# Hymba layer on one core: every on-chip tile begins on a multiple of 64 bytes of its partition

## The chip, the cores and the metric

The kernel runs on 1 core of one Trainium2 chip. The metric is device time in microseconds (us), the median of several runs; less is better. The engines are PE (TensorE, with PEld for its weight loads), DVE (VectorE), ACT (ScalarE), POOL (GpSimd) and SP (SyncE, which issues all DMAs here).

## What is computed

One layer on 2,048 rows of 1,024 float32 values: differential attention (4 heads) beside an HGRN2 recurrence (4 heads), an output projection, then a feed-forward part with a short convolution.

```python
h = _rmsnorm(x, ln1_w[l])
proj = h @ w_in[l]
dq, dk, dv, hq, hf, hi, hg = jnp.split(proj, offs, axis=-1)
...
o_diff = _diff_attention(dq, dk, dv, lam, lam_init, diff_subln_w[l])
...
o_hgrn = _hgrn2(hq, hf, hi, hg, lb, hgrn_norm_w[l])
x = x + jnp.concatenate([o_diff, o_hgrn], axis=-1) @ w_out[l]
x = x + _conv_ffn(_rmsnorm(x, ln2_w[l]), w_up[l], conv_w[l], conv_b[l], w_down[l])
```

`_conv_ffn` multiplies by `w_up` (1,024 x 5,632), convolves one half over 3 rows, applies silu, multiplies by the other half and then by `w_down` (2,816 x 1,024).

## The kernel before, in words

Every large product is made of three matmuls: each float32 operand is split into a high part and a remainder (`split` and `halves`, an ACT cast and a subtraction on DVE or POOL; the subtraction is line 582), and high x high, high x low and low x high are summed in PSUM. In `PE.matmul(dst, lhsT, rhs)`, lhsT is the stationary operand, loaded as weights, and rhs the moving one, streamed past it. The trace names a matmul `dst<-rhs,lhsT`.

There are four stages.
- **Mixer** (lines 157 to 485): four passes `s`, one for each pair of heads, each over eight blocks of 256 rows. `proj_a` multiplies a block hT (stationary) by WA (moving, 384 columns), `proj_b` by WB (256 columns), both through `mm3` (lines 215 to 225); `proj_c` has WC stationary and hT moving (256 columns, tile pjc). In each call `mm3` makes 8 x 3 matmuls; proj_a and proj_b are called for two row halves of a block, proj_c makes two products for the block. `attn` multiplies the queries qT by the keys kst into scores sc (lines 328 and 329, up to 512 columns each), reduces their maximum on DVE (333) and takes the exponential p on ACT (344). There is one score buffer, so that the next scores wait for p. `attn_o` transposes p (tpa, line 377, the moving operand is the identity), copies it to aT and multiplies it by the values vst (av, line 382; a plain float32 matmul, for which the trace holds two records). `hgrn` and `hgrn_o` make the recurrence in seven levels (lt, line 407). oo (line 390) and o1 (453) are stored to the DRAM tiles o_d.
- **Output projection** (lines 488 to 577): 16 blocks of 128 rows. `load_o` loads ot from o_d and xt from x, transposes ot (tpo, line 518) and splits it into oT; then 2 x 24 matmuls with oT stationary and the weights wo moving (pjo, lines 564 to 566, 512 columns). `tail` transposes the normed result (tph).
- **Up projection** (lines 580 to 687): a seven-product scheme over two row groups and 22 column tiles; each product has 12 matmuls (lines 648 to 650) with a weight tile WS stationary and an x tile (xB11, xT1, ...) moving, 512 columns: 2 x 22 x 7 x 12 = 3,696.
- **Down projection** (lines 690 to 836): the same scheme over four chunks `CH` of two or three row pairs `q` of w_down and eight row blocks: 8 x 7 x 11 x 3 = 1,848 matmuls (lines 770 to 772), SG stationary, TW moving, 512 columns. Line 717 puts the TW tiles of q = 2, 3, 6, 7 and 10 into the left-hand pool tl and those of q = 0, 1, 4, 5, 8 and 9 into the right-hand pool tr.

**Where the tiles lie.** Left-hand pools grow upwards from the constants, right-hand pools (`side="right"`) downwards from the end of the usable partition, byte 229344, which is 32 more than a multiple of 64. Tiles are rounded up to 32 bytes. So all large tiles of right-hand pools begin 32 bytes off a multiple of 64, and some on the left do so behind an odd tile (us, of 1,026 values, in pool wk3). First bytes of the tiles that matmuls read, in the program as built:

| operand | before | off 64 | changed |
|---|---|---|---|
| WA, WB, WC (moving WA, WB; stationary WC) | 37696, 62272, 78656 | 0 | 37952, 62528, 78912 |
| hT | 99104, 115488 | 32 | 96320, 112704 |
| kst, vst (moving), first of each | 198624, 219104 | 32 | 198592, 219072 |
| qT, aT (stationary), first of each | 146912, 163296 | 32 | 146880, 163264 |
| wo0 (moving), oT (stationary) | 37696, 115520 | 0 | 37952, 115776 |
| WS (stationary), first | 37696 | 0 | 37952 |
| xB11, xT1 (moving) | 163808, 196576 | 32 | 163776, 196544 |
| xB21, xT4, xB22 (moving) | 85024, 101408, 117792 | 32 | 85312, 101696, 118080 |
| TW left-hand (moving) | 37696 to 90944 | 0 | 37952 to 91200 |
| TW right-hand (moving) | 172000 to 225248 | 32 | 171968 to 225216 |
| SG (stationary), first | 121664 | 0 | 121920 |

The offsets within these tiles, of matmul operands, are multiples of 64 bytes but for the strided operands of line 407.

**What sets the order.** The instructions of each engine stand in a fixed order, which is made when the program is built: a scheduler takes them as their operands and their tiles come free. A tile that lies where an earlier pool had its own waits for that pool's tiles. The pools of the output projection (wp2, wk2, sm2) grow upwards from the left and end at byte 136320 before; the mixer's right-hand pools that reach down to them are hp (hT), pp, and above pp, from byte 138272 on, sm, which holds the scalars of a row and is in use until the mixer's last instruction. In the change sm begins at 135744 and sm2 ends at 136896.

```python
154      rw = pool(ctx, "rw", RB)
158          wp = pool(ms, "wp", 1)
161          wk = pool(ms, "wk", 2, side="right")
162          sm = pool(ms, "sm", 4, side="right")
163          pp = pool(ms, "pp", 2, side="right")
164          hp = pool(ms, "hp", 2, side="right")
491          wp = pool(ms, "wp2", 1)
492          wk = pool(ms, "wk2", 1)
493          sm = pool(ms, "sm2", 4)
```

Of the kernel before, what the change touches and what calls it, by code (L numbers as in the profile page):

```python
# [8 lines left out]
F32 = mybir.dt.float32  # L9
F32R = mybir.dt.float32r  # L10
BF16 = mybir.dt.bfloat16
U8 = mybir.dt.uint8
# [6 lines left out]
P = 128  # L19
# [2 lines left out]
ND = D // P  # L22
BLK = 256
NB = S // BLK
FF = 2816
NF = FF // P
EPS = 1e-6
# [6 lines left out]
NP = ("B11", "T2", "T1", "T3", "B21", "T4", "B22")  # L34
DP = ("B11", "B21", "T1", "T2", "T3", "T4", "B22")
CH = ((0, 1), (2, 3, 4), (5, 6, 7), (8, 9, 10))


@with_exitstack
def hymba_kernel(ctx, tc, x, ln1_w, w_in, q_norm_w, k_norm_w, lam_q1, lam_k1, lam_q2, lam_k2,  # L40
# [12 lines left out]
    conv_w = conv_w[0]  # L53

    def pool(stack, name, bufs, **kw):
        return stack.enter_context(tc.tile_pool(name=name, bufs=bufs, reuse_waits="tile", **kw))

    cst = ctx.enter_context(tc.tile_pool(name="cst", bufs=1))
    dram = ctx.enter_context(tc.tile_pool(name="dram", bufs=1, space=DRAM))

    ident = cst.tile([P, P], F32, name="ident")
    make_identity(nc, ident)
# [5 lines left out]
    def rstd(pool, ss, n, width, tag):  # L68
        m = pool.tile([P, n], F32, name=f"{tag}_m", tag=f"{tag}_m", bufs=3)
        POOL.tensor_scalar(out=m, in0=ss, scalar1=1.0 / width, scalar2=EPS, op0=ALU.mult, op1=ALU.add)  # L70
        r = pool.tile([P, n], F32, name=f"{tag}_r", tag=f"{tag}_r", bufs=3)
        POOL.tensor_tensor(out=r, in0=m, in1=mhalf[:, :n], op=ALU.pow)
        return r
# [73 lines left out]

    hT_d = [dram.tile([P, 2, ND, BLK], F32, name=f"hTd{b}") for b in range(NB)]
    o_d = [dram.tile([P, D], F32, name=f"od{t}") for t in range(S // P)]
    x2_d = [dram.tile([P, D], F32, name=f"x2d{t}") for t in range(S // P)]  # L150
    h2_d = [{n: dram.tile([P, 4, HG2], F32, name=f"h2d{b}{n}") for n in NP} for b in range(NS)]
    g_d = [[dram.tile([P, 2 * len(ch), BLK], F32, name=f"gd{u}_{c}") for c, ch in enumerate(CH)] for u in range(NU)]

    rw = pool(ctx, "rw", RB)

    # ---------------------------------------------------------------- mixer
    with ExitStack() as ms:
        wp = pool(ms, "wp", 1)
        kv = pool(ms, "kv", KVB, side="right")
        pb = pool(ms, "pb", PBB, side="right")  # L160
# [66 lines left out]
        for s in range(4):  # L227
# [239 lines left out]
            for c_ in ORDER if s else OF:  # L467
# [10 lines left out]
                elif s == 0 and c_ == "3":  # L478
                    load_prm(pa.tile([P, P], F32, name="tpp", tag="pj", bufs=PJB), pb.tile([P, P], F32, name="prm_r", tag="p"))
                    load_rest(pb.tile([P, D], F32, name="tmp", tag="p"), pb.tile([P, D], F32, name="tmq", tag="p"))  # L480
            for b in range(NB):
                for c_ in ORDER if s else O0:
                    nb_ = b + 1 + (c_ == "g" and s < GA) if c_ in "gABtuIJC" else b
                    if nb_ < NB:
                        step[c_](nb_)

    # ---------------------------------------------------------------- output projection
    up_st = ExitStack()
    hp = pool(up_st, "hp3", 1, side="right")
    with ExitStack() as ms:  # L490
# [85 lines left out]
            HTS[i] = ht  # L576
        tail(S // P - 1)

    # ---------------------------------------------------------------- conv GLU
    def halves(dst, src, eng):  # L580
        ACT.copy(dst[:, 0], src)  # L581
        eng.tensor_tensor(out=dst[:, 1], in0=src, in1=dst[:, 0].bitcast(F32), op=ALU.subtract)  # L582

    with up_st as ms:
# [53 lines left out]
        def up(b, f):  # L638
# [35 lines left out]
            DVE.tensor_tensor(out=c, in0=vs, in1=c, op=ALU.mult)  # L674
            ci = next(n for n, ch in enumerate(CH) if f // 2 in ch)
            for h in range(GRP // BLK):
                dma(out=g_d[GRP // BLK * b + h][ci][:, f - 2 * CH[ci][0], :], in_=c[:, h * BLK:(h + 1) * BLK])

# [7 lines left out]
            if f == NF - 1 and g + 1 < NS:  # L686
                load_h(g + 1)

    # ---------------------------------------------------------------- down projection
    with ExitStack() as ms:  # L690
        tr = pool(ms, "tr4", TRB, side="right")
        tq = pool(ms, "tq4", TWB, side="right")
# [28 lines left out]
        def prep_s(ci, u):  # L721
            nq = len(CH[ci])
            G = gp.tile([P, 6, BLK], F32, name="G", tag="G")
            dma(out=G[:, 0:2 * nq], in_=g_d[u][ci])
            Gv = G[:, 0:2 * nq].rearrange("p (q r) (m c) -> p r m q c", r=2, m=2)
            A11, A12, A21, A22 = Gv[:, 0, 0], Gv[:, 1, 0], Gv[:, 0, 1], Gv[:, 1, 1]

            def stile(a, b, op):
                t = sp.tile([P, 3, P], F32, name="sg", tag="sg", bufs=SGB)
                POOL.tensor_tensor(out=t[:, 0:nq], in0=a, in1=b, op=op)  # L730
                return t[:, 0:nq]

            S1 = stile(A21, A22, ALU.add)
            S2 = stile(S1, A11, ALU.subtract)
            S3 = stile(A11, A21, ALU.subtract)
            S4 = stile(A12, S2, ALU.subtract)
            out_ = []
            for src in (A11, A12, S1, S2, S3, A22, S4):
                w = sp.tile([P, 2, 3, P], F32R, name="SG", tag="SG", bufs=SSB)
                halves(w[:, :, 0:nq], src, DVE)  # L740
                out_.append(w)
            acc = []
            last = ci == len(CH) - 1 and u >= NU - NLU
            for m in range(2):
                if last:
                    a = tl.tile([P, D], F32, name="accl", tag="TW")
                    xr = tl.tile([P, D], F32, name="xrl", tag="TW")
                    dma(out=xr, in_=x2_d[2 * u + m])
                else:
                    a = ac.tile([P, D], F32, name="acc", tag="acc", bufs=ACB)  # L750
                if ci:
                    dma(out=a, in_=o_d[2 * u + m])
                if last:
                    DVE.tensor_tensor(out=a, in0=a, in1=xr, op=ALU.add)
                acc.append(a)
            GS[ci, u] = (out_, acc)
# [3 lines left out]
        def down(ci, u):  # L760
# [3 lines left out]
            def prod(n):  # L764
                pd = (ps, pa)[cnt[0] % 2].tile([P, 512], F32, name="pd", tag="pd")
                cnt[0] += 1
                qs = CH[ci]
                for k, q in enumerate(qs):
# [114 lines left out]
```

## Time and profile before

| what | value |
|---|---|
| median of 3 runs | 2836.1 us (2833.61 to 2836.53) |
| profiled execution: span | 2834.5 us |
| its own time | not listed apart; the span lies 1.6 us below the median |
| busy: PE, PEld | 2714.3 (96%), 2343.4 (83%) us |
| busy: DVE, ACT, POOL | 1982.5 (70%), 1199.8 (42%), 1093.0 (39%) us |
| DMA, mean | 117 GB/s |

The span is the time from the first to the last instruction of one execution. Busy time of PE is the time in which at least one matmul is under way; matmuls overlap their neighbours, so their durations add up to more than it.

### The profile page before, as it was taken

The page shows a single profiled execution, that of the slowest core. Times are in us where ns is not written, and L with a number is a line of the kernel's source. Part 1 is how long each engine was busy: PE and PEld are TensorE (multiplying, and loading weights), DVE is VectorE, ACT ScalarE, POOL GpSimd, SP SyncE. Part 2 cuts the span into 40 slices and gives each one's busy share as a digit, 9 for nine tenths or more (in the row PEclk, how much of TensorE's full clock was granted, in tenths as well). Part 3 has the DMA queues.
Part 4 walks back from the last instruction along what each step waited for, and adds up shares of the span by engine and source line. Part 5 has one row for each costly group of instructions (what it writes and reads, how often), then busy time and mean ns, then how long its engine had stood idle before and what let it go on. Part 6 is the DMA issues. An engine that isn't in the chain of part 4 may idle for free.

```text
span 2834.5 us, 42869 instructions
## 1 busy us (share of the span) xinstructions
PE 2714.3 (96%) x15298; PEld 2343.4 (83%) x15298; DVE 1982.5 (70%) x4049; ACT 1199.8 (42%) x2814; POOL 1093.0 (39%) x1137
## 2 busy tenths in 40 slices
PE   7999999999999999989999999999999998998988
PEld 6998999999999999978878888877888876786866
DVE  5677855785567656763347766687666669889898
ACT  4555534454345434443444434353333434333331
POOL 3322222222222222222144343334434347877775
PEclk9999999999999999999999999999999999999999
DMA  5223222131113111036763222244222224565665
GB/s 183 98 83 125 90 93 72 36 119 68 68 68 123 70 70 68 21 96 209 244 186 97 74 84 82 75 138 122 87 70 90 79 86 158 213 216 182 217 228 190
DMA packets 245556, 331.33 MB, mean 117 GB/s; under 512 B 16366, under 2 KB 203102, under 8 KB 241246
## 3 DMA queue, kind: packets, MB, share of 16 engines
q1 hardware_dynamic: 245342, 328.59, 34.6%
q8 instruction: 121, 1.98, 0.3%
q14 instruction: 93, 0.76, 0.1%
HBM read 223.67 MB, written 104.86 MB: 116 GB/s over the span
## 4 chain that ended last, share of the span: by engine, by line
PE 70%; DVE 14%; POOL 5%; ACT 4%; issue 4%; DMA 2%; SPq 0%; DVEq 0%; POOLq 0%; ACTq 0%
PE q L650 9%; PE q L649 9%; PE q L648 9%; PE pj L223 4%; PE pj L225 4%; PE pj L224 4%; PE av L382 3%; DVE SG L582 3%; PE lt L407 3%; DVE TW L582 2%; PE sc L328 2%; PE pjc L224 2%; PE pjc L223 2%; PE pjc L225 2%; PE pjo L564 2%
## 5 line engine op out<-in xcount | busy, mean ns | idle before, releaser
L648 PE MATMUL q<-xT,WS 128*128 128x512 f32 x704 | 279.6, 397 | 2.4 <-ACT xT L581 2.2
L770 PE MATMUL pd<-TW,SG 128*128 128x512 f32 x616 | 249.7, 406 | 33.5 <-DVE acc L776 13.5
L649 PE MATMUL q<-xT,WS 128*128 128x512 f32 x704 | 280.0, 398 | 1.5 <-DVE xT L582 1.5
L650 PE MATMUL q<-xT,WS 128*128 128x512 f32 x704 | 279.3, 397 | 0.4 <-DVE WS L582 0.4
L771 PE MATMUL pd<-TW,SG 128*128 128x512 f32 x616 | 249.0, 404 | 8.1 <-DVE TW L582 8.1
L772 PE MATMUL pd<-TW,SG 128*128 128x512 f32 x616 | 246.9, 402 | 1.6 <-DVE SG L582 1.5
L581 ACT CAST WS<-st 128x512 fp32r<-128x512 f32 x176 | 108.5, 618 | 253.7 <-PE q L650 239.4
L648 PE MATMUL q<-xB,WS 128*128 128x512 f32 x528 | 209.4, 397 | 1.6 <-ACT xB L581 1.6
L649 PE MATMUL q<-xB,WS 128*128 128x512 f32 x528 | 209.8, 397 | 1.1 <-DVE xB L582 1.1
L650 PE MATMUL q<-xB,WS 128*128 128x512 f32 x528 | 209.8, 398 | 0.9 <-DVE WS L582 0.9
L344 ACT ACTIVATE p<-sc,nm 128x1024 f32<-128x1024 f32 (+4 forms) x192 | 165.7, 863 | 98.8 <-DVE nm L333 97.8
L582 POOL TENSOR_TENSOR WS<-st,WS 128x512 fp32r<-128x512 f32 x44 | 91.5, 2078 | 287.6 <-ACT WS L581 266.6
L333 DVE TENSOR_REDUCE nm<-sc 128x1 f32<-128x1024 f32 (+4 forms) x192 | 174.3, 908 | 18.6 <-PE sc L329 16.3
L223 PE MATMUL pj<-WA,hT 128*128 128x384 f32 x512 | 176.3, 344 | 2.6 <-DVE hT L210 2.6
L225 PE MATMUL pj<-WA,hT 128*128 128x384 f32 x512 | 175.3, 342 | 0.0
L224 PE MATMUL pj<-WA,hT 128*128 128x384 f32 x512 | 175.2, 342 | 0.0
L770 PEld LDWEIGHTS pd<-TW,SG 128*128 128x128 f32 x616 | 119.0, 193 | 67.4 <-DVE acc L776 11.9
L582 DVE TENSOR_TENSOR WS<-rawu,WS 128x512 fp32r<-128x512 f32 x132 | 132.1, 1002 | 53.8 <-ACT WS L581 53.8
L648 PEld LDWEIGHTS q<-xT,WS 128*128 128x128 f32 x704 | 132.8, 189 | 35.3 <-ACT xT L581 2.7
L649 PEld LDWEIGHTS q<-xT,WS 128*128 128x128 f32 x704 | 132.6, 188 | 34.6 <-DVE xT L582 2.6
L650 PEld LDWEIGHTS q<-xT,WS 128*128 128x128 f32 x704 | 132.9, 189 | 33.0 <-DVE WS L582 0.9
L581 ACT CAST WS<-rawu 128x512 fp32r<-128x512 f32 x132 | 81.9, 622 | 177.6 <-PE q L650 177.3
(415 smaller groups left out, 7996.7 us busy)
## 6 DMA issues: line engine op xcount, KB each, us to landing
hT<-hTd SPq DMA_DIRECT2D x24, 2048.0 KB, 8.5
rawu<-in_w_up_dram SPq DMA_DIRECT2D x176, 256.0 KB, 3.1
od<-acc SPq DMA_DIRECT2D x48, 512.0 KB, 3.5
acc<-od SPq DMA_DIRECT2D x46, 512.0 KB, 4.6
gd<-c SPq DMA_DIRECT2D x176, 128.0 KB, 1.9
G<-gd SPq DMA_DIRECT2D x24, 768.0 KB, 5.6
xt<-in_x_dram SPq DMA_DIRECT2D x32, 512.0 KB, 4.0
hTd<-hT SPq DMA_DIRECT2D x8, 2048.0 KB, 7.6
```

The lines of the kernel that those rows point to most:

```text
L223: PE.matmul(dst, lhsT=lh, rhs=rh, start=dt == 0, stop=False)
L224: PE.matmul(dst, lhsT=lh, rhs=rl, start=False, stop=False)
L225: PE.matmul(dst, lhsT=ll, rhs=rh, start=False, stop=dt == ND - 1)
L333: DVE.tensor_reduce(out=nm, in_=sc[:, 0:w], axis=AX.X, op=ALU.max, negate=True)
L581: ACT.copy(dst[:, 0], src)
L582: eng.tensor_tensor(out=dst[:, 1], in0=src, in1=dst[:, 0].bitcast(F32), op=ALU.subtract)
L648: PE.matmul(dst, lhsT=w[:, 0, cs], rhs=b_[:, 0, dt], start=dt == 0, stop=False)
L649: PE.matmul(dst, lhsT=w[:, 0, cs], rhs=b_[:, 1, dt], start=False, stop=False)
L650: PE.matmul(dst, lhsT=w[:, 1, cs], rhs=b_[:, 0, dt], start=False, stop=dt == 3)
L770: PE.matmul(pd, lhsT=Sx[n][:, 0, k], rhs=w[:, 0], start=k == 0, stop=False)
L771: PE.matmul(pd, lhsT=Sx[n][:, 0, k], rhs=w[:, 1], start=False, stop=False)
L772: PE.matmul(pd, lhsT=Sx[n][:, 1, k], rhs=w[:, 0], start=False, stop=k == len(qs) - 1)
```

## The change

`Lines` wraps every pool in SBUF: it enlarges the first free dimension of a tile until its bytes are a multiple of 64, and hands out the part that was asked for. A row of one scalar thus takes 64 bytes, where it took 32. The pools in PSUM and DRAM are as before. A pool `top` takes the last 32 bytes of the right-hand side, so that what lies below it begins on multiples of 64. No instruction is added or left out. (The diff also drops four comment lines.) In the changed program all line numbers from `pool` on are higher by 19 to 22.

```diff
--- before.py
+++ after.py
@@ -22,6 +22,7 @@
 ND = D // P
 BLK = 256
 NB = S // BLK
+LINE = 64
 FF = 2816
...
+class Lines:
+
+
+    def __init__(self, pool):
+        self.pool = pool
+
+    def tile(self, shape, dt, **kw):
+        size = 1 if dt == U8 else 4
+        inner = 1
+        for n in shape[2:]:
+            inner *= n
+        n = shape[1]
+        while n * inner * size % LINE:
+            n += 1
+        t = self.pool.tile([shape[0], n, *shape[2:]], dt, **kw)
+        return t[:, 0:shape[1]] if n > shape[1] else t
...
     def pool(stack, name, bufs, **kw):
-        return stack.enter_context(tc.tile_pool(name=name, bufs=bufs, reuse_waits="tile", **kw))
-
-    cst = ctx.enter_context(tc.tile_pool(name="cst", bufs=1))
+        p = stack.enter_context(tc.tile_pool(name=name, bufs=bufs, reuse_waits="tile", **kw))
+        return p if "space" in kw else Lines(p)
+
+    cst = Lines(ctx.enter_context(tc.tile_pool(name="cst", bufs=1)))
     dram = ctx.enter_context(tc.tile_pool(name="dram", bufs=1, space=DRAM))
+    top = ctx.enter_context(tc.tile_pool(name="top", bufs=1, side="right"))
+    top.tile([P, 8], F32, name="edge")
```

The order of all engines is the one of before, but for one place: the seam between the mixer's last blocks and the output projection's first.

On SP, near the mixer's last stores: od_93 to od_108 are the o_d tiles of row blocks 0 to 15 in the program of before (od_97 to od_112 in the changed one), oo and o are what the mixer stores, ot the block that the output projection loads.

Before:

```order
L391 DMA od_107<-oo 128x128
L454 DMA od_107<-o_16231 128x128
L568 DMA x2d_109<-xt 128x1024
L512 DMA xt<-in_x_dram 128x1024
L454 DMA od_108<-o_16254 128x128
L510 DMA ot<-od_95 128x1024
L391 DMA od_108<-oo 128x128
```

Changed:

```order
L413 DMA od_111<-oo 128x128
L476 DMA od_111<-o_16235 128x128
L476 DMA od_112<-o_16258 128x128
L413 DMA od_112<-oo 128x128
L532 DMA ot<-od_97 128x1024
L534 DMA xt<-in_x_dram 128x1024 x2
L532 DMA ot<-od_98 128x1024
L590 DMA x2d_113<-xt 128x1024
```

Before, the result of row block 0 (x2d_109) and the load of block 2 (od_95) stand ahead of the mixer's last store; in the change, the load of block 0 (od_97) stands behind it.

On PE, where the output projection's first matmul stands (pjo; sc, lt, tpa, av and sp belong to the mixer):

Before:

```order
L328 MATMUL sc<-kst,qT 128x384
L329 MATMUL sc<-kst,qT 128x384
L407 MATMUL lt<-qP,kS 124x64 x2
L564 MATMUL pjo<-wo_16300,oT 128x512
L565 MATMUL pjo<-wo_16300,oT 128x512
L566 MATMUL pjo<-wo_16300,oT 128x512
```

Changed:

```order
L465 MATMUL sp<-ig,kt__16256 128x128
L399 MATMUL tpa<-ident,p 128x128 x8
L404 MATMUL av<-vst,aT 128x128 x8
L399 MATMUL tpa<-ident,p 128x128 x8
L404 MATMUL av<-vst,aT 128x128 x8
L540 MATMUL tpo<-ident,ot 128x128 x8
L586 MATMUL pjo<-wo_16304,oT 128x512
```

Before, the 48 matmuls of row block 0 begin in the middle of the last recurrence levels and are strewn among the mixer's rest; in the change, they and the transposes tpo stand behind the mixer's last av.

## Rows read from the trace of the kernel before

**Rows 1.** The chain of waits that ended last, as shares of the span by line.
```profile
by line: PE q L650 9.5%; PE q L649 9.4%; PE q L648 9.4%; PE pj L223 4.1%; PE pj L225 4.1%; PE pj L224 4.0%; issue 3.8%; PE av L382 3.5%; DVE SG L582 3.1%; PE lt L407 2.8%; DVE TW L582 2.2%; PE sc L328 2.1%; PE pjc L224 2.0%; PE pjc L223 1.9
```

**Rows 2.** Windows of mixer, seam, output, up and down projection; columns in line one.
```profile
core 0: us, PE busy (x) PEld busy (x) DVE busy (x) ACT busy (x) POOL busy (x), PEclk, DMA share, GB/s
...
40.00:1220.00 1180.00, 1145.34 (x8455) 1079.03 (x8455) 795.50 (x2581) 556.55 (x1600) 301.93 (x524) 1.00 0.23 82
1220.00:1270.00 50.00, 44.23 (x255) 38.10 (x256) 33.09 (x81) 21.39 (x54) 8.32 (x13) 0.88 0.25 77
1270.00:1455.00 185.00, 182.46 (x917) 153.06 (x916) 56.86 (x78) 68.94 (x178) 45.46 (x56) 1.00 0.65 209
1455.00:2345.00 890.00, 876.43 (x3719) 700.75 (x3719) 638.04 (x739) 368.06 (x598) 360.54 (x237) 0.99 0.31 95
2345.00:2835.00 490.00, 442.97 (x1835) 351.53 (x1833) 440.14 (x535) 165.45 (x348) 360.94 (x268) 0.96 0.57 202
```

**Rows 3.** Timeline, PE, output projection, 20 matmuls: start, us, engine, line.
```profile
1283.83 0.39 PE L565 MATMUL pjo<-wo,oT 128*128 128x512 f32 x1
...
1288.14 0.40 PE L566 MATMUL pjo<-wo,oT 128*128 128x512 f32 x1
```

**Rows 4.** Timeline, PE, up projection, first and last of 172 matmuls.
```profile
1699.92 0.40 PE L648 MATMUL q<-xB,WS 128*128 128x512 f32 x1
...
1739.90 0.40 PE L648 MATMUL q<-xB,WS 128*128 128x512 f32 x1
```

**Rows 5.** Timeline, PE, down projection: 40 matmuls of chunk 1, 64 of chunk 2.
```profile
2426.74 0.39 PE L772 MATMUL pd<-TW,SG 128*128 128x512 f32 x1
...
2435.88 0.40 PE L772 MATMUL pd<-TW,SG 128*128 128x512 f32 x1
...
2512.22 0.39 PE L771 MATMUL pd<-TW,SG 128*128 128x512 f32 x1
...
2526.69 0.39 PE L771 MATMUL pd<-TW,SG 128*128 128x512 f32 x1
```

**Rows 6.** Timeline, PE, mixer: 48 of WA then 24 of WB; 22 of pjc; tpa, av.
```profile
363.69 0.39 PE L223 MATMUL pj<-WA,hT 128*128 128x384 f32 x1
...
372.06 0.28 PE L223 MATMUL pj<-WB,hT 128*128 128x256 f32 x1
...
374.77 0.28 PE L225 MATMUL pj<-WB,hT 128*128 128x256 f32 x1
...
522.23 0.28 PE L225 MATMUL pjc<-hT,WC 128*128 128x256 f32 x1
...
524.71 0.28 PE L225 MATMUL pjc<-hT,WC 128*128 128x256 f32 x1
...
525.11 1.04 PE L377 MATMUL tpa<-ident,p 128*128 128x128 f32 x8
...
526.67 1.96 PE L382 MATMUL av<-vst,aT 128*128 128x128 f32 x16
```

**Rows 7.** The seam: timeline of ACT, PE, DVE; DMA issues; a window.
```profile
1232.02 0.19 ACT L344 ACTIVATION_READ_ACCUMULATOR p<-sc,nm 128x1 f32 x1
...
1233.80 0.40 PE L328 MATMUL sc<-kst,qT 128*128 128x512 f32 x1
...
1253.79 0.59 ACT L520 CAST oT<-tpo 128x512 fp32r<-128x512 f32 x1 [2.07 <-PE tpo L518]
...
1259.89 2.05 PE L382 MATMUL av<-vst,aT 128*128 128x128 f32 x16
...
1262.80 0.48 PE L564 MATMUL pjo<-wo,oT 128*128 128x512 f32 x1
...
1263.66 0.35 DVE L390 SCALAR_TENSOR_TENSOR oo<-av,fo,subw 128x128 f32<-128x128 f32 x1
...
ot<-od SPq DMA_DIRECT2D x16, 512.0 KB, 4.6
...
1218.00:1232.00 14.00, 7.91 (x25) 6.67 (x26) 12.41 (x30) 5.60 (x11) 3.79 (x4) 0.51 0.49 154
```

## The prediction

> **What bounds the kernel now.** I read the page first, then the stages as windows, then single matmuls in the timeline, and last the seam between mixer and output projection. The chain of waits that ended last runs through PE's matmuls in nearly all of its large lines [rows 1]. By stage [rows 2], PE is busy 1145 of 1180 us in the mixer, 182 of 185 in the output projection, 876 of 890 in the up projection, 443 of 490 in the down projection, where DVE's 440 lie close by. So outside the down projection the time is the number of matmuls times the step from the start of one to the start of the next. That step is the number to read; the duration printed for one matmul (0.40 us) overlaps its neighbours.
>
> The step depends on where the operands begin. All following matmuls have 512 moving columns.
> - Output projection: both operands begin on multiples of 64 (the placement table). 20 matmuls, 19 steps, 1283.83 to 1288.14: **0.2268 us** [rows 3].
> - Up projection: stationary WS on a multiple of 64, moving x tiles 32 off. 171 steps, 1699.92 to 1739.90: **0.2338 us** [rows 4].
> - Down projection, first chunk: all its TW tiles are right-hand ones, 32 off. 39 steps, 2426.74 to 2435.88: **0.2344 us**. Second chunk, where two row pairs of three have left-hand TW tiles on multiples of 64: 63 steps, 2512.22 to 2526.69: **0.2297 us** [rows 5]. Two thirds at 0.2268 and one third at 0.2340 would give 0.2292.
>
> The last pair is one line of code, one shape, one stage, with only the place of the tile changed. And the region of memory is not what decides: xB21 lies at 85024, among the left-hand TW tiles, and is in the slow set. The granted clock cannot explain it: it was 1.00 and 0.99 over the output and the up projection [rows 2].
>
> **The change, part by part.** It adds no instruction and drops none. It moves every tile to a multiple of 64, and, as the order of the program shows, it takes the start of the output projection out of the mixer's tail.
>
> *Up projection.* 2 x 22 x 7 x 12 = 3,696 matmuls, each with a moving operand that stops being 32 off: 0.2338 - 0.2268 = 7.0 ns, 26 us. PE is busy 876 of 890 us there, with DVE at 638, ACT at 368 and POOL at 361 [rows 2], so the whole of it lies on the path; a stage of about 865 us still leaves DVE over 220 us free. Bounds: -18, if a third of it turns into waits (PE idles 14 us there now), and -27, a little past the difference, since each start is printed to 0.01 us. I take **-25**, as the stage has some steps at its ends that no shorter read helps.
>
> *Mixer.* In the trace of before no 384- or 256-column matmul has both operands aligned, so I scale 0.2268 by the columns: 0.1701 and 0.1134. Measured: WA (384 columns, moving WA aligned, stationary hT 32 off) takes 8.37 us for 48 steps, 0.1744; WB (256, same operands' places) 2.71 us for 23 steps, 0.1178; pjc (256, moving hT 32 off, stationary aligned) 2.48 us for 21 steps, 0.1181 [rows 6]. Each kind has 4 x 8 x 2 x 8 x 3 = 1,536 matmuls: 4.3, 4.4 and 4.7 ns, together 20.6 us. The attention matmuls av (both operands off) take (1.96 - 0.28) / 15 = 0.112 us a step, the transposes tpa, whose moving identity is aligned, (1.04 - 0.27) / 7 = 0.110 [rows 6]: 2 ns on 1,088 records, 2.2 us. The 448 wide score matmuls, both off, I price like the up projection: 3.1 us. Sum 25.9 us. Not all is on the path: the chain holds 4.1% + 4.1% + 4.0% of 2834.5 us, 346 us, on the lines of WA and WB [rows 1], whose steps add up to 1536 x (0.1744 + 0.1178) = 449 us; that is 77%. I take **-20**; bounds -9 (the moving operands alone: 25.9 less 13.4 for WA and WB, of it 77%, rounded down) and -26 (all of it).
>
> *Down projection.* 1,848 matmuls; in six of eleven row pairs the moving tile was off, 1,008 matmuls, 7 ns each, 7 us. DVE is busy 440 of 490 us, PE 443 [rows 2]: I take about half, **-4**, bounds -1 and -7.
>
> *Output projection.* Its operands are aligned already: 0. *Other engines and DMA.* The tiles keep their sizes but for the scalars; I cost them at nothing: ACT, DVE and POOL wait for PE in three stages, and if one became slower by a hundredth, DVE's 638 us in the up projection would grow by 6 under a cover of 220.
>
> *The seam.* Before, SP loads ot for row block 0 ahead of the mixer's last stores, and PE does that block's transposes and its 48 matmuls in the gaps of the mixer's tail; the first matmul of block 1 starts at 1262.80, 0.9 us after the last av matmuls end (1259.89 + 2.05) [rows 7]. In the change, the load stands behind the last store of oo on SP, and the transposes and the 48 matmuls behind the last av on PE. Counted from the end of the last av: oo is written 2.1 us later (1263.66 + 0.35), the load takes 4.6 from issue to landing, four transposes half of the 1.04 that eight of tpa take [rows 6], the cast of the high part 0.6, of which I add two thirds again, 0.4, for the low part; then 48 x 0.2268 = 10.9, and eight transposes of block 1, 1.0. That is 20.1 us instead of 0.9, 19 later [rows 7]. SP, too, holds the loads of xt and the next ot behind that store, and ACT, DVE and POOL have nothing else to do meanwhile: nothing covers it. Against it: the tail itself ends sooner, since the 48 matmuls no longer stand between the scores; by the gap between the end of p at 1232.2 and the score matmul at 1233.80 [rows 7], some 2 to 4 us. [...] I take **+20**, bounds +13 and +27.
>
> Sum: -25 - 20 - 4 + 20 = **-29 us** on the profiled execution's span of 2834.5. The runs' median, 2836.1, lies 1.6 above it; I carry this over: 2836.1 - 29 = **2807 us**.
>
> [...]
>
> [...]
>
> **The rivals.**
> - *A, slower.* The steps differ for another reason that stays (the tile's neighbours, the stage's other traffic); only the seam is left: 2836 + 20 = 2856. For: nowhere in the mixer is an aligned pair to compare with. Against: the two chunks of the down projection [rows 5]. It decides below the point where the alignment gives less than the seam's 20 us, that is, below 20 of the 49 us, or 3 ns for a matmul of 512 columns. 6%.
> - *B.* Only moving operands count: WA and WB give nothing, 0.77 x 13.4 = 10 us less: 2817. For: no row shows the place of a stationary operand alone, at one shape; 0.1701 and 0.1134 are scaled. 17%.
> - *C.* The seam costs little, because the tail without the 48 matmuls is much shorter and the clock stays up: +8 instead of +20: 2795. For: PE was busy 44 of 50 us from 1220 to 1270 [rows 2], a quarter of it with the moved 48 matmuls. Against: the tail's chain goes through scores, maxima and exponentials, each waiting for the one before. 14%.
> - *D.* In the up projection a chain through ACT, DVE and POOL becomes the bound, and half of its 25 us is lost: 2820. Against: DVE 638 of 890. 8%.
> - The forecast: 55%.
>
> **How the numbers follow.** The forecast's own bounds are -27 - 26 - 7 + 13 = -47 and -18 - 9 - 1 + 27 = -1 us, if all fall together, 2789 to 2835; its likely part is 2794 to 2822. B, C and D stand inside that. The range, 2790 to 2826, takes in these and leaves out A and the slow end, where several terms would have to fail at once. A change under 0.2%, 5.7 us, can hardly be told from none by a measurement of this kernel. Faster by more than that: 0.88 (all of the forecast, B, C and D but their slow ends); within it: 0.06; slower: 0.06 (A).
>
> **What would show it.** Right: steps in the up projection of 0.227 as in the output projection, the first and second chunk of the down projection at one step, WA near 0.170 and WB and pjc near 0.113; at the seam a stretch of some 7 us without matmuls before block 0's first, and block 1's first matmul some 20 us further behind the last av. Wrong: the up projection still at 0.234 (A), WA and WB unchanged beside a faster pjc (B), matmuls close behind the last av (C), or new waits of PE for DVE or ACT in the up projection (D).

## The result: slower by 20 us, and what the profile after shows

The changed kernel takes 2856.2 us (median of 4 runs, 2854.4 to 2860.2), the kernel before 2836.3 beside it; ratio 1.0072, 95% interval 1.0058 to 1.0087. The profiled execution took 2855.5 us, its span 2853.8, 19.3 above that of before. Forecast were 2807 and a gain.

Where the 19.3 us came from is read from five starts in the two traces: the last pjc of the mixer, the first pjo of row block 1 (1262.80 before [rows 7], 1291.56 after, below), the first q, the first pd, the last pd (2827.49 and 2846.78). The other three, and the first matmul with WA of the mixer's second pass, first before, then after:

```profile
311.21 0.34 PE L223 MATMUL pj<-WA,hT 128*128 128x384 f32 x1
...
1203.70 0.28 PE L225 MATMUL pjc<-hT,WC 128*128 128x256 f32 x1
...
1454.82 0.40 PE L648 MATMUL q<-xB,WS 128*128 128x512 f32 x1
...
2339.65 0.51 PE L770 MATMUL pd<-TW,SG 128*128 128x512 f32 x1 [3.27 <-ACT SG L581]
```

```profile
313.09 0.34 PE L245 MATMUL pj<-WA,hT 128*128 128x384 f32 x1
...
1206.18 0.28 PE L247 MATMUL pjc<-hT,WC 128*128 128x256 f32 x1
...
1484.18 0.40 PE L670 MATMUL q<-xB,WS 128*128 128x512 f32 x1
...
2359.42 0.50 PE L792 MATMUL pd<-TW,SG 128*128 128x512 f32 x1 [3.49 <-ACT SG L603]
```

| stage | forecast, us | measured, us |
|---|---|---|
| mixer, to the last pjc | -20 | +2.5 |
| seam, to the first pjo of block 1 | +20 | +26.3 |
| rest of the output projection | 0 | +0.6 |
| up projection | -25 | -9.6 |
| down projection | -4 | -0.5 |

Two windows after, the seam and the up projection (columns as in [rows 2]):

```profile
1220.00:1270.00 50.00, 32.34 (x161) 27.83 (x161) 30.39 (x78) 16.64 (x40) 9.13 (x12) 0.66 0.14 40
...
1485.00:2357.00 872.00, 859.62 (x3702) 696.55 (x3702) 634.74 (x731) 362.67 (x586) 350.32 (x231) 0.99 0.31 95
```

From 1220 to 1270 PE is busy 32 us where it was 44, at a mean granted clock of 0.66 where it was 0.88 [rows 2]. That is the seam. The up projection is shorter, but by 10 us and not 25. Its timeline shows why. Below are the first and last of 36 matmuls with left-hand moving tiles (xB21, xT4, xB22), then of the 48 with right-hand ones (xB11, xT2, xT1, xT3) that follow (start, us, engine, line):

```profile
1700.37 0.39 PE L670 MATMUL q<-xB,WS 128*128 128x512 f32 x1
...
1708.32 0.39 PE L672 MATMUL q<-xB,WS 128*128 128x512 f32 x1
1708.54 0.40 PE L670 MATMUL q<-xB,WS 128*128 128x512 f32 x1
...
1719.51 0.39 PE L672 MATMUL q<-xT,WS 128*128 128x512 f32 x1
```

Left: 7.95 us in 35 steps, 0.2271, as forecast. Right: 10.97 in 47 steps, 0.2334, as before [rows 4]. Both begin on multiples of 64 now. In the down projection, 64 matmuls of the second chunk:

```profile
2504.18 0.40 PE L793 MATMUL pd<-TW,SG 128*128 128x512 f32 x1
...
2518.74 0.40 PE L793 MATMUL pd<-TW,SG 128*128 128x512 f32 x1
```

14.56 us for 63 steps, 0.2311; a stretch of one forecast 0.2268, and it was 0.2297 before the change [rows 5]. And the mixer, 48 matmuls of WA, 24 of WB, then 13 of pjc:

```profile
365.61 0.39 PE L245 MATMUL pj<-WA,hT 128*128 128x384 f32 x1
...
373.82 0.33 PE L247 MATMUL pj<-WA,hT 128*128 128x384 f32 x1
373.99 0.28 PE L245 MATMUL pj<-WB,hT 128*128 128x256 f32 x1
...
376.74 0.28 PE L247 MATMUL pj<-WB,hT 128*128 128x256 f32 x1
...
524.39 0.28 PE L245 MATMUL pjc<-hT,WC 128*128 128x256 f32 x1
...
525.83 0.28 PE L245 MATMUL pjc<-hT,WC 128*128 128x256 f32 x1
```

WA 8.21 / 47 = 0.1747, WB 2.75 / 23 = 0.1196, pjc 1.44 / 12 = 0.120; before 0.1744, 0.1178 and 0.1181 [rows 6]. Nothing was gained in these stretches, and the narrow ones lost 2 ns each. But most of the mixer's 2.5 us came earlier: the second pass begins 1.9 us later than before, behind a stretch in which the granted clock was lower in the one profiled execution, a mean of 0.94 where it was 1.00 (first before, then after):

```profile
40.00:100.00 60.00, 55.62 (x407) 52.98 (x408) 35.78 (x128) 28.07 (x84) 16.78 (x30) 1.00 0.31 114
```

```profile
40.00:100.00 60.00, 56.06 (x390) 53.85 (x389) 33.67 (x119) 27.32 (x83) 16.73 (x30) 0.94 0.32 115
```

From the second pass on, where the clock is 1.00 in every trace up to the last pjc, the mixer is 0.6 us longer than before. The experiments' traces differ in their first 100 us likewise, by 0 to 10 us at the lower clock (a granted 0.50; the traces of before and after show 0.50 and 1.00 and no other), and their second pass begins between 0.7 us earlier and 2.9 later than before; so the time of their last pjc alone is no measure of 1 or 2 us.

The seam, on PE and for one row DVE:

```profile
1261.42 3.56 PE L404 MATMUL av<-vst,aT 128*128 128x128 f32 x16
...
1266.09 2.05 PE L404 MATMUL av<-vst,aT 128*128 128x128 f32 x16 [0.24 <-ACT aT L401]
1274.48 1.97 PE L540 MATMUL tpo<-ident,ot 128*128 128x128 f32 x8 [6.34 <-DMA ot<-od]
1276.99 0.79 PE L586 MATMUL pjo<-wo,oT 128*128 128x512 f32 x1 [0.55 <-DVE oT L543]
...
1281.42 0.52 PE L587 MATMUL pjo<-wo,oT 128*128 128x512 f32 x1
...
1290.20 0.60 PE L540 MATMUL tpo<-ident,ot 128*128 128x128 f32 x4
...
1291.56 0.47 PE L586 MATMUL pjo<-wo,oT 128*128 128x512 f32 x1
```

```profile
1269.83 0.35 DVE L412 SCALAR_TENSOR_TENSOR oo<-av,fo,subw 128x128 f32<-128x128 f32 x1
```

From the end of the last av, 1268.14: oo written 2.0 us later, the load's landing 4.3 after that, transposes and casts 2.5, the 48 matmuls 13.2, two groups of four transposes 1.4: 23.4 us, where 0.9 stood before [rows 7]. Forecast were 20.1, by the same steps; most of the rest is the clock, which stood at its lower level for the transposes and the first ten matmuls (a granted 0.50 from 1271.4 to 1281.6; 4.43 us for ten, 0.443 each, in place of 0.227).

### The profile page after: what moved, and what is told of

Same layout as the page of the kernel before. It is cut to its first block, busy times and chain, and to the rows that moved or that the text cites. A ratio compares the mean times of both kernels' runs of the same rounds, so it can differ in the third digit from the quotient of the medians.

```text
span 2853.8 us, 42874 instructions
## 1 busy us (share of the span) xinstructions
PE 2716.8 (95%) x15298; PEld 2357.4 (83%) x15298; DVE 1981.9 (69%) x4049; ACT 1200.1 (42%) x2814; POOL 1095.1 (38%) x1137
## 4 chain that ended last, share of the span: by engine, by line
PE 72%; DVE 13%; POOL 5%; ACT 4%; issue 3%; DMA 3%; SPq 0%; DVEq 0%; POOLq 0%; ACTq 0%
PE q L671 9%; PE q L672 9%; PE q L670 9%; PE pj L245 4%; PE pj L247 4%; PE pj L246 4%; PE av L404 3%; DVE SG L604 3%; PE lt L429 3%; PE sc L350 2%; PE pjc L246 2%; DVE TW L604 2%; PE pjc L245 2%; PE pjc L247 2%; PE pjo L586 2%
```

## The experiments

The question: both sides of the change, the alignment and the order, came out differently. Since every tile lies where its pool puts it, small strips of unused bytes move whole groups of tiles. The theories, as the expectations number them: 1, alignment is worth little and the order costs 26 to 29 us; 4, the step of a matmul goes by the distance between its moving and its stationary operand, modulo 256 bytes; against them 2, 3, 5, 6 and 7. In the expectations "xT" stands for the four right-hand moving tiles of the up projection (2,112 matmuls) and "xB" for the three left-hand ones (1,584). Every kernel but the second, the ninth and the tenth has the order of the kernel before on every engine; those three have that of the changed one. Means of steps are taken over all following starts of one kind in the trace, without those over 1.12 times the median, which are waits.

**1. Alignment without the order.**

```diff
-        while n * inner * size % LINE:
+        while n * inner * size > LINE // 2 and n * inner * size % LINE:
```

> Edit: whole 64-byte lines only for tiles of more than 32 bytes a partition; the scalar tiles of the mixer keep 32 bytes. The order of every engine is then that of the kernel before, and every matmul operand still begins on a multiple of 64. It separates alignment from order. Theory 1 (alignment is worth little: by the trace after, up gains 9.8 us, down 0.5, the mixer loses 2.5; the loss of 26 to 29 us is the seam's order): 2836.3 - 9.8 - 0.5 + 2.5 = about 2828, between 2824 and 2832, up stage 9 to 11 us shorter than before, the mixer to the last pjc within 3 us of before. Theory 2 (alignment is worth the 49 us that were forecast, and the changed order takes 69): about 2787. Theory 3 (alignment is worth nothing at all): 2836.

Measured: 2821.0 us, ratio 0.9943 (0.9927 to 0.996). Up is 12.0 us shorter than before (9 to 11 expected), down 0.2, the seam 0.6; right-hand steps in up 233.1 ns, left-hand ones 227.2. The mixer's last pjc comes 3.3 us earlier, and not later, so the time lies 3 us under theory 1's band. Theories 2 and 3 fall: 2821 is neither 2787 nor 2836.

**2. The order without the alignment.**

```diff
+        while n * inner * size <= LINE // 2 and n * inner * size % LINE:
...
-    top = ctx.enter_context(tc.tile_pool(name="top", bufs=1, side="right"))
-    top.tile([P, 8], F32, name="edge")
```

> Edit: the other half: only the tiles of up to 32 bytes take 64, and no strip stands at the end of the right side. The order of every engine is that of the kernel after, while the matmul operands that were 32 off before are 32 off again. Theory 1: the seam alone, +26 to +29 us, 2862 to 2866, with the first pjo of block 1 some 26 to 29 us later than before and up and down steps as before (up xT mean 234, down 231.4). Theory 2 (the order takes 69): about 2905. A third reading (the seam's delay comes from the aligned mixer, which runs at another pace into it): 2836 to 2845.

Measured: 2862.1 us, 1.0087 (1.0072 to 1.0102), inside theory 1's band by its lower edge. Block 1's first pjo comes 25.1 us later than before; all later stages keep their lengths within 0.6 us. On PE:

```profile
1262.77 2.05 PE L402 MATMUL av<-vst,aT 128*128 128x128 f32 x16 [0.24 <-ACT aT L399]
1270.86 1.97 PE L538 MATMUL tpo<-ident,ot 128*128 128x128 f32 x8 [6.04 <-DMA ot<-od]
1273.38 0.79 PE L584 MATMUL pjo<-wo,oT 128*128 128x512 f32 x1 [0.55 <-DVE oT L541]
...
1287.87 0.47 PE L584 MATMUL pjo<-wo,oT 128*128 128x512 f32 x1
```

The chain is the one above: from the end of the last av, 1264.82, to 1287.87 are 23.1 us, 23.4 there. Counted from the last pjc, the seam is 24.8 us longer than before. The change's 26.3 came with 3.4 us more at the lower clock between the same two starts (44.4 and 41.0 us). So the seam's loss is the order's; of the alignment no part is seen in it.

**3 and 4. Another distance.** The right side 128 and 64 bytes lower.

```diff
-    top.tile([P, 8], F32, name="edge")
+    top.tile([P, 40], F32, name="edge")
```

(24 in place of 40 in the fourth.)

> Edit: as the first of these runs, but the strip at the end of the right side is 160 bytes in place of 32, so that everything on the right lies 128 bytes lower; all is still on multiples of 64. The tiles xT11, xT1, xT2, xT3 of up and the right-hand TW of down then begin at 64 past a multiple of 256, as the stationary tiles WS and SG do, in place of 192. In the trace after, up's matmuls with moving data at 64 past step 226.7 ns, those at 192 past 229 or 237 (mean 233). Theory 4 (the step goes by the distance between moving and stationary operand modulo 256, none being best): up's xT matmuls go to 226.7, 2112 x 6.3 ns = 13 us less than in the first run, down's right-hand ones to 227, 1008 x 5 ns = 5 us less, and the left-hand ones recover with them, 840 x 4 ns = 3.4 us: about 2828 - 21 = 2807. Theory 5 (no rule of that kind, the step is set by something else): within 3 us of the first run, 2825 to 2831.

> Edit: the same with a strip of 96 bytes: the right side 64 bytes lower than in the first run, its tiles in up and down at 128 past a multiple of 256, a distance of 64 from the stationary ones. Theory 4: not the best distance, so the steps of up's xT stay above 226.7 (between 229 and 237), the time between 2812 and 2835. Theory 6 (192 past is a bad place by itself, whatever the stationary one does, and 128 past a good one): up's xT at 226.7, 2807. Theory 5: 2825 to 2831.

Measured: 2809.9 us, 0.9904 (0.9889 to 0.9919), and 2822.7 us, 0.9948 (0.9933 to 0.9963). Up in the third, 48 right-hand matmuls, then 36 left-hand ones:

```profile
1694.88 0.39 PE L670 MATMUL q<-xB,WS 128*128 128x512 f32 x1
...
1705.53 0.39 PE L672 MATMUL q<-xT,WS 128*128 128x512 f32 x1
1705.76 0.39 PE L670 MATMUL q<-xB,WS 128*128 128x512 f32 x1
...
1713.69 0.39 PE L672 MATMUL q<-xB,WS 128*128 128x512 f32 x1
```

10.65 / 47 and 7.93 / 35: 0.2266 for both, and up is 24.4 us shorter than before. In the fourth, 48 right-hand ones:

```profile
1699.81 0.40 PE L670 MATMUL q<-xB,WS 128*128 128x512 f32 x1
...
1710.58 0.39 PE L672 MATMUL q<-xT,WS 128*128 128x512 f32 x1
```

10.77 / 47 = 0.2291, and 229.3 ns over all; up is 17.4 us shorter than before, while the last pjc comes 3.7 later. Theory 4 stands for up, theories 5 and 6 fall (128 past is not a good place). But theory 4's 8.4 us in the down projection came as 1.1 in the third (1.2 less than before, where the first run had 0.2 less): its steps fell to 227.2 (right) and 227.0 (left), a free stretch of the second chunk to 14.28 us for 63 steps:

```profile
2473.59 0.39 PE L793 MATMUL pd<-TW,SG 128*128 128x512 f32 x1
...
2487.87 0.39 PE L793 MATMUL pd<-TW,SG 128*128 128x512 f32 x1
```

and PE waited longer for what it multiplies with. What ended PE's idle time before pd (us, times), first in the kernel before, then in the third run, the four largest:

```profile
  DVE acc L776: 13.5, 4
  DVE V L776: 9.1, 3
  DVE TW L582: 8.1, 3
  ACT V L803: 5.3, 3
```

```profile
  DVE acc L798: 13.7, 4
  DVE V L798: 10.6, 5
  DVE TW L604: 7.9, 3
  ACT V L825: 7.5, 4
```

Together 36.0 and 39.7 us. Against before, the steps gave 1008 x 6.2 + 840 x 2.0 ns = 7.9 us; 3.7 of them are seen again in these four rows. Most of the rest may be the clock: PE stood at a granted 0.50 for 43.1 us of the stage, 37.5 before, and half of these 5.6 us is 2.8, an estimate of the most that it costs. The waits are rival D's mechanism, in the stage where the prediction had allowed for it.

**5 and 6. Is it the place or the distance, and does 64 matter at all?** In the fifth the right side stays as in the first run and the left side moves; in the sixth no large operand begins on a multiple of 64, and the distances in up, down, output projection and scores are all 0.

```diff
+    cst.tile([P, 32], F32, name="shift")
```

and

```diff
+    cst.tile([P, 8], F32, name="shift")
...
-    top.tile([P, 8], F32, name="edge")
+    top.tile([P, 32], F32, name="edge")
```

> Edit: the first run's kernel (strip of 32 bytes on the right), with 128 bytes more at the beginning of the left side. The right-hand tiles stay at 192 past a multiple of 256, where up's xT took 229 to 237 ns; the left-hand ones (WS, SG, xB, the left TW, wo) go from 64 to 192. Theory 4 (the distance between moving and stationary operand modulo 256 counts, not the place of either): all these distances are 0 now, so up and down step as in the third run, 226.8 and 227 ns for all of them, although nothing lies where it lay there; 2810, up stage 24 us shorter than before. Theory 6 (192 past is a bad place for the moving operand by itself): xT stays at 233 and xB joins it, 1584 x 6 ns = 9.5 us more than the first run, 2830. Mixer under theory 4: hT at 0, WA at 192, the distance of the third run, so the last pjc as there (203.5 past 1000).

> Edit: the first run's kernel with 32 bytes more at the beginning of the left side, and 128 in place of 32 at the end of the right: every large operand of up, down, output projection and scores begins at 96 past a multiple of 256, so none on a multiple of 64, and all distances between moving and stationary are 0 modulo 256. Theory 4: as the third run, steps of 226.8 to 227.2 in up and down, 2810. Theory 7 (the change's own idea, starts on multiples of 64 are what a matmul wants, and the distance comes on top): 230 or more in all of them, the output projection's 227 lost as well, 2825 to 2845.

Measured: 2811.8 us, 0.9913 (0.9898 to 0.9928), and 2811.9 us, 0.9915 (0.99 to 0.9929). The sixth's up projection, 48 right-hand and 36 left-hand matmuls, all of them 32 off:

```profile
1694.36 0.39 PE L671 MATMUL q<-xB,WS 128*128 128x512 f32 x1
...
1705.02 0.39 PE L673 MATMUL q<-xT,WS 128*128 128x512 f32 x1
1705.24 0.39 PE L671 MATMUL q<-xB,WS 128*128 128x512 f32 x1
...
1713.18 0.39 PE L673 MATMUL q<-xB,WS 128*128 128x512 f32 x1
```

10.66 / 47 = 0.2268 and 7.94 / 35 = 0.2269; up 24.6 us shorter than before, in the fifth 23.4. That settles it for up: the place of an operand does not count by itself (64, 96 and 192 past a multiple of 256 all step 226.7 to 226.8), and a multiple of 64 does not count. Theories 6 and 7 fall. In the third, fifth and sixth runs the right-hand tiles lie at distances that are multiples of 512 from the stationary ones, xB21, xT4 and xB22 at odd multiples of 256, and both step 226.7; a distance of 128 took 233. So it is modulo 256.

**7. The last distance, and the mixer at the place it has after the change.** The strip is `[P, 56]`.

> Edit: a strip of 224 bytes: right-hand tiles of up and down at 0 past a multiple of 256, 64 below the stationary ones, and hT of the mixer at 64, where the kernel after has it, with the order of the kernel before. Theory 4: up's xT between 228 and 234, as at the distance of +64 (229.3 there); down as there; and the mixer, with hT and W both at 64, as in the kernel after: WB and pjc near 119.4, the last pjc 2 to 4 us later than before; 2820 to 2830. If the mixer's loss in the kernel after came from its order and not from the distance, the last pjc is within 1 us of before.

Measured: 2825.6 us, 0.9964 (0.9952 to 0.9977). 48 right-hand matmuls of up:

```profile
1699.74 0.39 PE L670 MATMUL q<-xB,WS 128*128 128x512 f32 x1
...
1710.70 0.39 PE L672 MATMUL q<-xT,WS 128*128 128x512 f32 x1
```

10.96 / 47 = 0.2332. The distance of -64 costs as much as 128. WB and pjc step 119.4 and 119.2, the last pjc comes 1.8 us later than before, somewhat under the 2 to 4 expected. From the second pass on, at full clock, the mixer took 892.5 us before; it takes 0.6 to 0.9 more where hT is at distance 0 (the change, runs 7 and 10), 2.4 to 2.6 less at 64 (runs 1 and 8), between 1.4 less and 0.8 more at 128 and 192, and 1.7 less in run 2, which has the changed order at a distance of 224. So this loss goes with hT's distance and not with the order, but it is under 1 us; the other part of the 1.8 us came in the first pass. All distances together, up, 512 columns:

| moving less stationary, modulo 256 | step, ns | where |
|---|---|---|
| 0 | 226.7 to 226.8 | runs 3, 5, 6, 8, 9 |
| 64 | 229.3 | run 4 |
| 128 | 233.1 | the change, run 1 |
| 160 | 234.2 | before, right-hand tiles |
| 192 | 233.3 | run 7 |
| 224 | 233.3 | before, left-hand tiles |

For 256 columns it is another table. WB, by W less hT: 119.4 at 0, 117.1 at 32 (before), 117.6 to 117.8 at 64, 118.6 to 118.7 at 128, 115.8 to 116.2 at 192, 118.2 at 224 (run 2). The steps of pjc, where hT moves and WC is stationary, agree with it within 0.3 ns when they are put down by hT less W (119.2 to 119.4 at 0, 117.0 at 32, 115.9 to 116.4 at 192). WA, 384 columns, lies between 173.3 and 176.0 at all of them.

One kind does not follow the first table: the scores' wide matmuls (sc, 512 columns) have distance 0 in all twelve programs and step 231.0 to 232.5. They come in bursts of four or fewer between matmuls of other tiles, so that they may never settle at the step of a long run (see the down projection below); no run parts this.

**8. The best of both.** The third run with 128 bytes more above hT in the mixer.

```diff
+        gap = pool(ms, "gap", 1, side="right")
+        gap.tile([P, 32], F32, name="gap")
         hp = pool(ms, "hp", 2, side="right")
```

> Edit: the third run's kernel with 128 bytes more above hT in the mixer, so that hT lies at 0 past a multiple of 256 there, as in the first run, where the mixer was 3.3 us shorter than before; all else as in the third run. Theory 4 (stages add up, each by its own distance): the third run less 3 us, 2806 to 2808, the last pjc 3 us earlier than before and up as in the third run. If the mixer's 3 us are something else (the place of the scores' operands, or chance): 2810.

Measured: 2808.9 us, 0.9902 (0.9888 to 0.9917), the last pjc 1.1 us earlier than before, up 23.1 us shorter. It is the lowest time of the study, 28 us under the kernel before, but not to be told from the third run. In the mixer, WA, WB and pjc step as in the first run (173.3, 117.8 and 116.4; 173.3, 117.6 and 115.9 there), and from the second pass on it is 2.4 us shorter than before, as the first run was (2.6). What is missing of the 3 us lies in the first pass, with 10.2 us at the lower clock. So the mixer's gain is there, and the time of the whole is too coarse to show it.

**9 and 10. The sum, and the source of the order.** The ninth is the changed kernel with `[P, 40]` for its strip; the tenth is the first run with whole lines for the mixer's pool sm alone (`0 if name in ('sm',) else LINE // 2` as the size up to which a tile is left as it is).

> Edit: the changed kernel, with one number different: the strip at the end of the right side has 160 bytes in place of 32. The order of every engine is that of the changed kernel. Theory 4 with the order's loss as a term of its own: the third run's 2810 plus the 25 us that the order alone cost, 2835, between 2831 and 2839, that is, no difference from before that could be told; up steps of 226.8 ns, up and down together 23 to 27 us shorter than before. If the order's loss and the distances get in each other's way (the loss is smaller where the stages after it are faster): below 2830.

> Edit: the first run's kernel, but the scalars of the mixer's pool sm (nm, l, ss1, r1 and the like, 78 tiles of 32 bytes) take 64 bytes; those of pp and sm2 keep 32. The order of every engine is then that of the changed kernel. If the pool sm's growth of 2.5 KB is all that the seam's loss comes from: the first run's 2821 plus 25 to 29, 2846 to 2852 with block 1's first pjo 23 to 28 us later than before. If the growth of pp or sm2 is needed for the loss as well: 2821 to 2840.

Measured: 2840.9 us, 1.0018 (1.0008 to 1.0027), and 2853.5 us, 1.0059 (1.0042 to 1.0076). Both are a little above their bands. In the ninth, up is 24.2 us shorter than before and the seam 27.0 longer, so these two add up. The rest of the output projection is 2.3 us longer there and 1.8 in the tenth, each with 3.4 us at the lower clock. In the ninth the strip also puts hT at a distance of 128 (WA 176.0, WB 118.7), as in run 4, which the expectation overlooked; but the last pjc comes 2.3 us later by the first pass alone, and from the second pass on the mixer is as long as before. In the tenth, hT lands at distance 0, the last pjc 1.5 us later and not 3.3 earlier as in the first run, a difference of 4.8 that was overlooked likewise (3.2 of it from the second pass on). The seam takes 26.0 us more than before (last pjc at 1205.18, first pjo of block 1 at 1290.24) with sm's growth alone. That growth, 78 tiles times 32 bytes, is enough for all of the loss.

## Why the prediction was wrong, step by step

- **"Any operand that is 32 off costs 7 ns" was the step that failed.** It was read from [rows 3 to 5], and the steps were read rightly. But each pair that was called aligned there was also at distance 0 modulo 256 (wo and oT both at 64, left-hand TW and SG both at 64), and each that was called misaligned was not (x tiles at 32 and 224, right-hand TW at 224, against WS and SG at 64). Two causes lay in the same rows, and I took the one that the change named. The fixed control that I offered, the same line and shape with only the tile's place changed, moved both. Run 6 parts them: 32 off at distance 0 takes 0.2268. So the cost was put on the wrong property: it goes by the distance between moving and stationary operand modulo 256 bytes (226.7 ns at 0, 233.1 at 128 in up).
- **Up, -25, measured -9.6.** The left-hand tiles went from distance 224 to 0 and gave 1584 x 6.1 ns = 9.7 us. The right-hand ones went from 160 to 128, 234.2 to 233.1, 2.2 us. Of these 11.9 us, 2.3 are not seen; run 1, with the same steps, was 12.0 shorter, and the changed kernel's trace stood at the lower clock for 10.2 us of the stage, run 1's for 4.5. The forecast's sum was right for another placement: the third run's -24.4.
- **Mixer, -20, measured +2.5.** Here the targets 0.1701 and 0.1134 were scaled from 0.2268 by the columns, and that was wrong by itself. With distance 0 the steps are 0.2267, 0.173 (the commonest of WA after the change) and 0.120: 53 to 54 ns apart for each 128 columns, which leaves about 13 ns of the 120 that the columns do not account for, an estimate from these three. WA and WB had little to give: their best means in any run are 173.3 and 115.8, against 174.6 and 117.1 before. hT at distance 0 even cost WB and pjc 2 and 1 ns, and from the second pass on the stage was 0.6 us longer; the other 1.9 us came in the first pass, with the clock.
- **Down, -4, measured -0.5.** The half that was allowed for DVE was right in kind: even run 3, with all steps at 227, got 1.2. But the change gave no faster step to begin with (right 233.4 to 232.0, left 229.0 to 231.1). Its left-hand tiles lay at distance 0 before and after; a matmul's step thus depends on its neighbours' too. The up projection shows the same: of its 36 left-hand matmuls, at distance 0, the first three behind the right-hand ones step 231 to 233 ns in the change and the first ten 224 to 236 in run 4, and only the following ones 226.7.
- **Seam, +20, measured +26.3, bound +27.** The chain was right link by link (20.1 forecast, 23.4 measured). The +20 also holds a part of 3 to 6 us for a lower clock, a term of my own that no run shows. What the runs showed in its place, between the last pjc and block 1's first pjo, is a granted 0.50 for 44.4 us in the change and for 13.7 before (a mean of 0.51 from 1218 to 1232 [rows 7]); the first ten matmuls behind the wait took 4.43 us, where ten steps of 0.227 are 2.27. What went over is the clock and the tail, which was to end 2 to 4 us sooner and, counted from the last pjc to the last av, ended 3.7 later (2.6 in run 2). From 1220 to 1270, with PE busy 32 of 50 us, the granted clock was a mean of 0.66, and the scores and av ran slower where it stood at 0.50: the scores from 1235.33 on step 0.42 to 0.43 us, those from 1246.03 on, at full clock, 0.23; the 16 records of av at 1261.42 take 3.56 us, the 16 at full clock behind them 2.05.
- **Rival A** gave the right number, 2856, by luck: its sum is the seam alone, at 20 us, and measured were 26.3 there, 2.5 in the mixer and -9.6 in up. Its sentence was half right: most step differences stayed, and for another reason than the start of the tile, but not those of up's left-hand tiles. It had 6%, because the two chunks of the down projection seemed to exclude it. Rival B, that only moving operands count, is wrong as it stands: neither operand's place counts.
- **Starts that are 32 off** cost nothing by themselves: with both operands 32 off at distance 0, up's steps are 0.2268 and 0.2269 (run 6). And the stationary operand is a part of the distance: up's right-hand steps go from 233.1 to 226.8 when only the left side moves, the stationary tiles with it (runs 1 and 5).

Still open: why the step repeats every 256 bytes of the two operands' distance; whether the stationary operand that counts is the matmul's own or the next one's, whose load overlaps it (in the up projection of before PEld is busy 700.75 of 890 us while PE is busy 876.43 [rows 2]; all stationary tiles of a stage lay at the same place modulo 256 in every run); and which of the mixer's scalar tiles under which tile of the output projection makes the program hold row block 0 back. None of the three was tried apart.

## What to carry to other kernels

Before a difference between rows is put down to a property, list what else differs between the same rows; here the placement table already held both columns, the operand's own offset and its distance to the other one, and only one was looked at. Place moving and stationary tiles of long runs of wide matmuls (512 columns) at equal offsets modulo 256: a strip of 160 bytes in place of 32 was worth 11 us here (run 1 to run 3). And look at the order after each change of a tile's size: growing a few scalars by 2.5 KB cost 25 us, where all that the rest of the change gave, with that order out of the way, was 16 (run 1).

## What was not expected of the hardware

- In the up projection the step of a 512-column matmul (float32r tiles, which the trace prints as f32) goes from 226.7 to 234.2 ns with the distance of its two operands modulo 256 bytes, at a granted clock of 0.99 to 1.00 over the stage; at distance 0 it is 226.7 whether both operands lie on multiples of 64 or both 32 off. It takes three to ten matmuls behind others at another distance to come to that value.
- The dependence differs with the width: 256-column matmuls of WB were slowest (119.4) where 512-column ones are fastest, and fastest (115.8 to 116.2) at a distance of 192, where those take 233.3.
- The slow steps are no scatter: in the change, 39% of the right-hand steps in up are 229 ns and 46% are 237 or 238, in turns, each matmul of the pattern of 12 with its own value time after time.
- With the 48 matmuls that the kernel before keeps in the gaps of the mixer's tail, the granted clock is higher: a mean of 0.88 from 1220 to 1270 with them [rows 2], 0.66 without. From the last pjc to the last av it is 0.88 to 0.91 in the eight kernels that have them there and 0.72 to 0.75 in the four that do not.
